# Another opening for a hybrid attention block: x turned by products with a diagonal, and the first key projection by halves of the tokens

## The chip, the cores and the metric

The kernel runs on one core of one Trainium2 chip. The time is device microseconds of one execution, input and output in DRAM; the figure that counts is the median of several runs. One execution of the kernel before was also taken by the hardware profiler, and all rows shown here are of it. The engines are named as in its page: PE (TensorE matmul), PEld (the loading of PE's stationary operand), DVE (VectorE), ACT (ScalarE), POOL (GpSimd) and SP (SyncE, which here only issues DMAs).

## The reference, cut to what matters

The reference is one layer of a block with 512 tokens and 1024 features. The change touches its first steps:

```python
xn = rmsnorm(x, n_mix_pre)           # x * rsqrt(mean(x*x) + eps) per token, times one weight per feature
proj = xn @ w_in                     # 1024 x 14352
qa, ka, va, za, beta_logit, a_dt, qb, kb, vb, gb, gate_a, gate_b = _split_cols(proj, IN_SIZES)
...
qkv = jax.nn.silu(causal_depthwise_conv(jnp.concatenate([qa, ka, va], axis=-1), conv_a))
...
beta = jax.nn.sigmoid(beta_logit)
g = -jnp.exp(a_log) * jax.nn.softplus(a_dt + dt_bias)
```

beta_logit and a_dt are 8 columns each, columns 6144 to 6159 of w_in; the keys ka are columns 1024 to 2047. After these come a gated delta rule over 8 heads, a retention over 4 heads, gates, an output projection and an MLP, all unchanged here.

## The kernel before, in words

Products with weights are made in three parts: each float32 operand is split into a high part of the matmul's own float32r type and a low part that is the rest, and `mm3` (lines 82 to 87) adds high by high, high by low and low by high in PSUM (the lines L84, L85, L86 of the profile). `weights` (L88) issues on SP's queue the load of a block of 512 KB into one of two buffers `raw` (L94), then `split_weights` makes `whi` on ACT (L121) and `wlo` on DVE (L122), each in a ring of three buffers. A block for the keys is 2 groups of 128 features of x by 512 columns, so a block feeds 4 x 2 x 3 = 24 matmuls and four blocks make the first 512 key columns.

The order on each engine is made by a scheduler when the program is built: it follows dependences and priorities, and each engine then runs its own list strictly in that order. The list of SP decides when loads are issued; a load of a block waits until the buffer that it fills has been read.

The opening (L399 to L507) works like this:

- The norm weight of 4 KB goes to one partition (`wrow`, L401), and two float32 matmuls with a row of ones spread it over 128 partitions in two PSUM banks (`wmix`, L406).
- Eight bf16 matmuls on zeros (`warm`, L413) run on PE before data has come.
- SP loads x in four tiles of 128 tokens (L417), then a block of 128 columns from column 6144 for beta and the decay (512 KB, of which 16 columns are used), then the key blocks. ACT's queue loads `cmat` (192 KB: an identity, a triangle and a mask, L419); POOL's queue loads five small tensors (L422 to L427).
- For each pair of tiles ACT squares and sums (L434), and `root` (L375 to L385) makes the norm's factor per token, its square root on ACT at L379, the rest on DVE.
- For each tile DVE makes `xn`, x times factor times weight, in two halves (L444); `rows_to_features` turns it by transposes on PE (L363) four at a time; ACT rounds each four to the high part (L396), DVE makes the low part (L397). The results are the two `actT` tiles, `xs` in the code.
- After each pair the beta/decay matmuls run, 24 of 256 tokens into a PSUM tile of 128 rows (`pba`).
- The chain of beta and decay follows (L463 to L507): a copy on ACT (`baT`, L466), small transposes (L469), exponentials and a logarithm with three table loads on ACT, and tiny DVE steps.
- Then `keys(0, ...)` calls `feature_major` (L287), which runs the four key blocks with 96 matmuls of all 512 tokens. `conv_silu` (L539) takes each of the four results: ACT copies (L544) and scales (L549), DVE makes three taps (L551) and so on. The matmul with `tg` at L575 is the first on PE that does not belong to the first keys or the opening.

`seen` and `passed` (L76) are rows of 48 numbers; each mark is a copy of one number by ACT (L105) and by POOL (L106), after which a DMA that adds in DRAM is issued. From the load numbered 13 on, `weights` also issues DRAM to DRAM copies from a list (`trickle`, L98), one for each load.

Of the kernel before, what the change touches and what calls it, by code (L numbers as in the profile page):

```python
# [10 lines left out]
F32 = mybir.dt.float32  # L11
F32R = mybir.dt.float32r
# [3 lines left out]
ALU = mybir.AluOpType  # L16
# [3 lines left out]
P = 128  # L20
T = 512
D = 1024
# [3 lines left out]
OFF_BA = 6144  # L26
# [34 lines left out]
def hybrid_block_kernel(ctx: ExitStack, tc: tile.TileContext, a: dict, out: bass.AP):  # L61
    nc = tc.nc
# [10 lines left out]
    marks = itertools.count()  # L73
    act = ctx.enter_context(tc.tile_pool(name="act", bufs=2))
    sm = ctx.enter_context(tc.tile_pool(name="sm", bufs=2))
    seen, passed = (sm.tile([1, 48], F32, tag=f"mark{i}", name="mark", bufs=1) for i in range(2))  # L76
    psm = ctx.enter_context(tc.tile_pool(name="psm", bufs=4, space=PSUM))
    psx = ctx.enter_context(tc.tile_pool(name="psx", bufs=4, space=PSUM))
    dr = ctx.enter_context(tc.tile_pool(name="dr", bufs=2, space=DRAM))
# [1 line left out]
    def mm3(ps, lhs, rhs, first, last):  # L81
        lh, ll = lhs
        rh, rl = rhs
        nc.tensor.matmul(ps, lh, rh, start=first, stop=False)  # L84
        nc.tensor.matmul(ps, lh, rl, start=False, stop=False)  # L85
        nc.tensor.matmul(ps, ll, rh, start=False, stop=last)  # L86
# [310 lines left out]
            nc.vector.tensor_tensor(dst[1][:, ks, tt], ps, dst[0][:, ks, tt], ALU.subtract)  # L397

    with tc.tile_pool(name="xp", bufs=2) as xp:  # L399
        wrow = xp.tile([1, D], F32, name="wrow", bufs=1)  # L400
        nc.scalar.dma_start(wrow, a["norm_mix_pre"][0:1, :])  # L401
        one = xp.tile([1, P], F32, name="one", bufs=1)
        nc.vector.memset(one, 1.0)
        wmix = [psm.tile([P, T], F32, tag="mm", name="wmix") for _ in range(2)]
        for half in range(2):
            nc.tensor.matmul(wmix[half], one, wrow[:, half * T : half * T + T], start=True, stop=True)  # L406
        warm = xp.tile([P, T], BF16, name="warm", bufs=1)
        nc.vector.memset(warm, 0.0)
        first = xp.tile([1, 1], F32, name="first", bufs=1)
        nc.scalar.activation(first, one[:, 0:1], AF.Sqrt)  # L410
        pw = psx.tile([P, T], F32, tag="dl", name="dl", bufs=3)
        for _ in range(8):
            nc.tensor.matmul(pw, warm[:, 0:P], warm, start=True, stop=True)  # L413
        xts = []
        for t in range(4):
            xt = xp.tile([P, D], F32, tag="x", name="x", bufs=4)
            nc.sync.dma_start(xt, x_d[t * P : (t + 1) * P, :])  # L417
            xts.append(xt)
        nc.scalar.dma_start(cmat, a["c_mat"])  # L419
# [8 lines left out]
        pba = [psm.tile([P, 256], F32, tag="mm", name="mm") for _ in range(2)]  # L428
        rx = []
        for pair in range(2):  # L430
            v = xp.tile([P, 2], F32, tag="xv", name="xv")
            for i in range(2):
                junk = xp.tile([P, D], BF16, tag="junk", name="junk")
                nc.scalar.activation(junk, xts[2 * pair + i], AF.Square, accum_out=v[:, i : i + 1])  # L434
            nc.vector.tensor_scalar(v, v, 1.0 / D, EPS, ALU.mult, ALU.add)
            y = root(v)
            rx += [y[:, i : i + 1] for i in range(2)]
            if pair == 0:
                wh, wl = weights(w_in, 0, 8, OFF_BA, P)
        for t in range(4):  # L440
            xn = xp.tile([P, D], F32, tag="xn", name="xn")
            for half in range(2):
                hs = slice(half * T, half * T + T)
                nc.vector.scalar_tensor_tensor(xn[:, hs], xts[t][:, hs], rx[t], wmix[half], ALU.mult, ALU.mult)  # L444
            rows_to_features(xn, t, xs)
            if t % 2:
                tt = slice((t - 1) * P, (t + 1) * P)
                for kt in range(8):
                    mm3(
                        pba[t // 2],  # L450
                        (wh[:, kt, :], wl[:, kt, :]),
                        (xs[0][:, kt, tt], xs[1][:, kt, tt]),
                        kt == 0,
                        kt == 7,
                    )
# [4 lines left out]
        nc.vector.tensor_scalar(convw, pv[:, 1, :], 0.5, None, ALU.mult)  # L460
        nc.scalar.copy(later, cmat[:, 2 * P : 3 * P])


        baT = xp.tile([16, T], F32, tag="baT", name="baT")
        for i in range(2):
            nc.scalar.copy(baT[:, i * 256 : i * 256 + 256], pba[i][0:16, :])  # L466
        pb = psx.tile([P, 4, P], F32, tag="tr", name="tr", bufs=1)
        for c in range(4):
            nc.tensor.transpose(pb[:, c, 0:16], baT[:, c * P : (c + 1) * P], ident[0:16, 0:16])  # L469
        ba = xp.tile([P, 4, 16], F32, tag="ba", name="ba")  # L470
        nc.vector.tensor_copy(ba, pb[:, :, 0:16])
        nc.scalar.activation(beta, ba[:, :, 0:8], AF.Exp, scale=-1.0)
# [36 lines left out]
    def gate_rows(pss, o_t, zt):  # L509

# [79 lines left out]
    with tc.tile_pool(name="pa", bufs=1) as pa:  # L590
# [9 lines left out]
        def keys(g4, pool):  # L600
# [700 lines left out]
```

## Time and profile before

| what | value |
|---|---|
| median of 3 runs | 1380.97 us (1379.35, 1380.97, 1384.16) |
| the profiled execution's own time | 1381.27 us |
| its span, first to last instruction | 1379.3 us |
| PE busy | 1357.4 us, 98% of the span |
| DVE, ACT, POOL busy | 953.5, 647.9, 149.0 us |
| DMA | 230.42 MB, mean 167 GB/s |

The profiled execution took 2.0 us more than its span, and lies 0.3 us above the median. In rows of the timeline the first number is the start in us from the span's start, the second the length; what stands in brackets is how long the engine was idle before, and what ended that. Matmuls are pipelined, so the rate of a stream is read from start to start, not from the length of a row. A float32 matmul is recorded twice.

### The profile page before, as it was taken

The page shows a single profiled execution, that of the slowest core. Times are in us where ns is not written, and L with a number is a line of the kernel's source. Part 1 is how long each engine was busy: PE and PEld are TensorE (multiplying, and loading weights), DVE is VectorE, ACT ScalarE, POOL GpSimd, SP SyncE. Part 2 cuts the span into 40 slices and gives each one's busy share as a digit, 9 for nine tenths or more (in the row PEclk, how much of TensorE's full clock was granted, in tenths as well). Part 3 has the DMA queues.
Part 4 walks back from the last instruction along what each step waited for, and adds up shares of the span by engine and source line. Part 5 has one row for each costly group of instructions (what it writes and reads, how often), then busy time and mean ns, then how long its engine had stood idle before and what let it go on. Part 6 is the DMA issues. An engine that isn't in the chain of part 4 may idle for free.

```text
span 1379.3 us, 17789 instructions
## 1 busy us (share of the span) xinstructions
PE 1357.4 (98%) x6574; PEld 1107.1 (80%) x6574; DVE 953.5 (69%) x1631; ACT 647.9 (47%) x1198; POOL 149.0 (11%) x218
## 2 busy tenths in 40 slices
PE   8999999999999999999999999999999999999997
PEld 6888788787887888888888888878878888888885
DVE  5599889963675557567477577575776757395688
ACT  5777564634453323454453343343355544353443
POOL 1112200221012001201001002010001101100000
PEclk9999999999999999999999999999999999999999
DMA  5243625469358447977476477582659847765563
GB/s 161 67 148 108 202 74 170 130 137 237 105 124 173 115 145 201 249 235 193 117 222 158 133 195 147 160 243 77 184 212 293 207 127 223 159 188 162 184 196 123
DMA packets 108281, 230.42 MB, mean 167 GB/s; under 512 B 7616, under 2 KB 21074, under 8 KB 107683
## 3 DMA queue, kind: packets, MB, share of 16 engines
q1 hardware_dynamic: 89424, 177.76, 40.3%
q0 software_dynamic: 18048, 50.29, 19.2%
q10 hardware_dynamic: 722, 1.25, 0.2%
q8 instruction: 51, 0.84, 0.2%
q14 instruction: 36, 0.29, 0.1%
HBM read 221.40 MB, written 74.97 MB: 215 GB/s over the span
## 4 chain that ended last, share of the span: by engine, by line
PE 83%; DVE 8%; DMA 5%; ACT 2%; issue 1%; POOL 1%; SPq 0%; DVEq 0%; ACTq 0%
PE mm L86 17%; PE mm L85 16%; PE mm L84 16%; PE mm L281 13%; PE dl L281 10%; DMA raw<-in_w_in_dram 3%; PE tr L363 2%; DVE wlo L122 1%; ACT whi L121 1%; PE dl L86 1%; PE dl L85 1%; PE dl L84 1%; DVE c_y L551 1%; PE dl L815 1%; DMA raw<-in_w_out_dram 1%
## 5 line engine op out<-in xcount | busy, mean ns | idle before, releaser
L122 DVE TENSOR_TENSOR wlo<-raw,whi 128x1024 fp32r<-128x1024 f32 x262 | 320.0, 1223 | 275.8 <-ACT whi L121 274.1
L121 ACT CAST whi<-raw 128x1024 fp32r<-128x1024 f32 x262 | 275.1, 1051 | 462.5 <-PE mm L85 257.5
L86 PE MATMUL mm<-actT,wlo 128*128 128x512 f32 (+1 forms) x528 | 209.1, 396 | 0.0
L85 PE MATMUL mm<-actT,whi 128*128 128x512 f32 (+1 forms) x528 | 208.0, 394 | 1.0 <-DVE actT L397 1.0
L84 PE MATMUL mm<-actT,whi 128*128 128x512 f32 (+1 forms) x528 | 207.7, 395 | 0.6 <-ACT actT L396 0.6
L84 PEld LDWEIGHTS mm<-actT,whi 128*128 128x128 f32 x528 | 100.5, 191 | 20.5 <-ACT actT L396 1.0
L85 PEld LDWEIGHTS mm<-actT,whi 128*128 128x128 f32 x528 | 100.4, 190 | 20.3 <-DVE actT L397 1.3
L86 PEld LDWEIGHTS mm<-actT,wlo 128*128 128x128 f32 x528 | 100.7, 191 | 18.7
L84 PE MATMUL mm<-hn,whi 128*128 128x512 f32 (+1 forms) x288 | 106.9, 371 | 0.5 <-DVE fr L1200 0.5
L86 PE MATMUL mm<-hn,wlo 128*128 128x512 f32 (+1 forms) x288 | 106.7, 371 | 0.0
L85 PE MATMUL mm<-hn,whi 128*128 128x512 f32 (+1 forms) x288 | 106.6, 370 | 0.0
L84 PE MATMUL mm<-og,whi 128*128 128x512 f32 x256 | 99.8, 390 | 0.3 <-DVE zz L514 0.3
L85 PE MATMUL mm<-og,whi 128*128 128x512 f32 x256 | 99.7, 390 | 0.0
L86 PE MATMUL mm<-og,wlo 128*128 128x512 f32 x256 | 99.7, 390 | 0.0
L281 PE MATMUL mm<-whi,xsum 128*128 128x512 f32 x256 | 82.3, 395 | 0.0
L281 PE MATMUL mm<-whi,fsum 128*128 128x512 f32 x240 | 77.2, 395 | 0.0
L106 POOL COPY mark<-mark 1x1 f32<-1x1 f32 x42 | 33.2, 791 | 395.0 <-ACT mark L105 388.0
L551 DVE SCALAR_TENSOR_TENSOR c_y<-c_raw,convw,c_y 128x512 f32<-128x512 f32 x96 | 70.0, 745 | 3.5 <-ACT c_y L549 2.8
L84 PEld LDWEIGHTS mm<-hn,whi 128*128 128x128 f32 x288 | 54.2, 188 | 10.8 <-issue 0.7
L85 PEld LDWEIGHTS mm<-hn,whi 128*128 128x128 f32 x288 | 54.3, 188 | 10.1
L86 PEld LDWEIGHTS mm<-hn,wlo 128*128 128x128 f32 x288 | 54.2, 188 | 10.0
L84 PE MATMUL mm<-whi,actT 128*128 128x512 f32 x152 | 61.4, 404 | 0.1
(339 smaller groups left out, 2588.0 us busy)
## 6 DMA issues: line engine op xcount, KB each, us to landing
raw<-in_w_in_dram SPq DMA_DIRECT2D x105, 512.0 KB, 3.8
raw<-sums SPq DMA_DIRECT2D x64, 512.0 KB, 4.0
raw<-in_w_up_dram SPq DMA_DIRECT2D x36, 512.0 KB, 6.7
sums<-in_w_in_dram SPq DMA_DIRECT2D x32, 512.0 KB, 5.3
sums<-sums POOLq DMA_DIRECT2D x32, 512.0 KB, 7.7
sums<-in_w_down_dram SPq DMA_DIRECT2D x32, 512.0 KB, 7.1
raw<-in_w_down_dram SPq DMA_DIRECT2D x24, 512.0 KB, 4.5
raw<-in_w_br_a_dram SPq DMA_DIRECT2D x16, 512.0 KB, 4.2
```

What stands on the lines that cost most here:

```text
L84: nc.tensor.matmul(ps, lh, rh, start=first, stop=False)
L85: nc.tensor.matmul(ps, lh, rl, start=False, stop=False)
L86: nc.tensor.matmul(ps, ll, rh, start=False, stop=last)
L106: mark = nc.gpsimd.tensor_copy(passed[:, k : k + 1], seen[:, k : k + 1])
L121: nc.scalar.copy(hi[:, :n], raw[:, :n])
L122: nc.vector.tensor_tensor(lo[:, :n], raw[:, :n], hi[:, :n], ALU.subtract)
L281: m = nc.tensor.matmul(pss[t], lhs[i // 2], rhs[i % 2], start=first and k + i == 0, stop=k + i == 5, skip_group_check=not first,)
L363: nc.tensor.transpose(ps, src, ident)
L551: nc.vector.scalar_tensor_tensor(y, raw[:, j : j + T], tap(j), y, ALU.mult, ALU.add)
L815: nc.tensor.matmul(po[:, hh, :], at[:, 4 * hh + c, :], vn[:, hh, :], start=True, stop=True)
```

## The change

The transposes of the normed x are replaced. The factor of each token is put on the diagonal of a 128 x 128 matrix (`diag`, one DVE operation with the identity), and a float32 matmul with 128 features of x as the stationary operand and that diagonal as the moving one gives the turned and scaled tile. The norm's weight then belongs to the partition: it comes as 8 rows of 128 (`wm_in`), is turned once on PE into a column per group of features (`wcol`), and is applied as a scale when ACT and DVE split the turned tile (`split_from`, 256 tokens at a time, 8 for each pair). `wmix`, `xn` and `rows_to_features` are not used in the opening any more.

The beta/decay weights are loaded as 16 columns (64 KB in pieces of 64 bytes) between the second and the third tile of x; high and low part stand side by side as 32 columns of one stationary operand, so 2 matmuls of 256 tokens take the place of 3, and a DVE addition joins the two halves later. The first keys are made by halves of 256 tokens: three blocks of weights are kept in the ring while the first half runs, the second half follows after the beta/decay matmuls, and the fourth block runs both halves at once. The identity is loaded ahead of the rest of `cmat`, which goes behind x on SP's queue. 16 zero matmuls stand where 8 stood. The rows of marks have 64 numbers. The number of blocks that `weights` counts is one smaller from here on.

```diff
-    seen, passed = (sm.tile([1, 48], F32, tag=f"mark{i}", name="mark", bufs=1) for i in range(2))
+    seen, passed = (sm.tile([1, 64], F32, tag=f"mark{i}", name="mark", bufs=1) for i in range(2))
...
-        wmix = [psm.tile([P, T], F32, tag="mm", name="wmix") for _ in range(2)]
-        for half in range(2):
-            nc.tensor.matmul(wmix[half], one, wrow[:, half * T : half * T + T], start=True, stop=True)
...
+        nc.scalar.dma_start(ident, a["c_mat"][:, 0:P])
...
-        for _ in range(8):
+        for _ in range(16):
             nc.tensor.matmul(pw, warm[:, 0:P], warm, start=True, stop=True)
...
+            nc.sync.dma_start(xts[t], x_d[t * P : (t + 1) * P, :])
+            if t == 1:
+                nc.sync.dma_start(
+                    wba, w_in[:, OFF_BA : OFF_BA + 16].rearrange("(k p) c -> p k c", p=P)
+                )
+        nc.sync.dma_start(cmat[:, P : 3 * P], a["c_mat"][:, P : 3 * P])
...
+                diag = xp.tile([P, P], F32, tag="diag", name="diag", bufs=4)
+                nc.vector.tensor_scalar(diag, ident, y[:, i : i + 1], None, ALU.mult)
...
+                        nc.tensor.matmul(
+                            ps[:, kk, i * P : (i + 1) * P],
+                            xts[2 * pair + i][:, k * P : (k + 1) * P],
+                            diags[i],
...
+                    split_from(ps[:, kk, :], xs[0][:, k, tt], xs[1][:, k, tt], wcol[:, k : k + 1])
...
+        token_features(0)
+        wba2 = xp.tile([P, 8, 32], F32R, name="wba2", bufs=1)
...
+        beta_decay(0)
+        kept = [key_weights(0), key_weights(1)]
+        first_keys(0, kept[0], [0])
+        token_features(1)
...
+        first_keys(1, kept[1], [0])
+        kept.append(key_weights(2))
+        first_keys(2, kept[2], [0])
+        beta_decay(1)
...
+        for k2 in range(3):
+            first_keys(k2, kept[k2], [1])
+        first_keys(3, key_weights(3), [0, 1])
...
-            pss = feature_major(w_in, xs, OFF_KA + g4 * 512, 512, 8)
+            pss = pss or feature_major(w_in, xs, OFF_KA + g4 * 512, 512, 8)
...
-            keys(0, pa2)
+            keys(0, pa2, pk0)
```

ACT's list from the squares of the first two tiles (`junk,xv<-x`) to the last high part of x (`actT`), in the kernel before; `whi` is the rounding of a block of weights:

```order
L434 ACTIVATE junk,xv<-x 128x1024 x2
L461 CAST later<-cmat 128x128
L379 ACTIVATE nr_y<-xv 128x2
L434 ACTIVATE junk,xv<-x 128x1024 x2
L396 CAST actT<-tr 128x4x128
L379 ACTIVATE nr_y<-xv 128x2
L121 CAST whi<-raw 128x1024
L396 CAST actT<-tr 128x4x128 x3
L121 CAST whi<-raw 128x1024 x2
L466 COPY baT<-mm 16x256
L396 CAST actT<-tr 128x4x128 x4
```

The same place in the changed kernel, where the fourth tile's square stands between the first and the second of the first pair's eight splits:

```order
L379 ACTIVATE nr_y<-xv 128x2
L441 ACTIVATE junk,xv<-x 128x1024
L346 ACTIVATE actT<-tr,wcol 128x256
L441 ACTIVATE junk,xv<-x 128x1024
L346 ACTIVATE actT<-tr,wcol 128x256 x3
L121 CAST whi<-raw 128x1024
L346 ACTIVATE actT<-tr,wcol 128x256 x3
L121 CAST whi<-raw 128x1024
L379 ACTIVATE nr_y<-xv 128x2
L502 CAST later<-cmat 128x128
L346 ACTIVATE actT<-tr,wcol 128x256
L121 CAST whi<-raw 128x1024
```

The root of the second pair (the second `nr_y`) has moved behind two roundings of weights and six more splits; the second pair's eight splits follow the third rounding.

PE's list in the kernel before, around the transposes of the second pair's third and fourth tile (`tr<-cmat,xn`); `mm<-actT,whi` of 256 tokens is beta/decay, of 512 tokens the first keys:

```order
L363 MATMUL tr<-cmat,xn 128x128 x12
L469 MATMUL tr<-cmat,baT 128x16 x2
L84 MATMUL mm<-actT,whi 128x256
L84 MATMUL mm<-actT,whi 128x512 x2
L363 MATMUL tr<-cmat,xn 128x128 x4
L84 MATMUL mm<-actT,whi 128x512
L363 MATMUL tr<-cmat,vecs_in 128x128
L85 MATMUL mm<-actT,whi 128x256
```

All but three of the 96 key matmuls of 512 tokens stand behind the last transposes of x.

In the changed kernel `tr<-diag,x` are the products with the diagonal and `mm` of 256 tokens are key matmuls; these rows begin at the last key matmuls ahead of the second pair:

```order
L481 MATMUL mm<-actT,whi 128x256 x2
L481 MATMUL mm<-actT,wlo 128x256
L481 MATMUL mm<-actT,whi 128x256
L455 MATMUL tr<-diag,x 128x128 x12
L481 MATMUL mm<-actT,whi 128x256
L481 MATMUL mm<-actT,wlo 128x256
L481 MATMUL mm<-actT,whi 128x256 x2
L481 MATMUL mm<-actT,wlo 128x256
L481 MATMUL mm<-actT,whi 128x256
L455 MATMUL tr<-diag,x 128x128 x4
```

Ahead of the second pair's products PE now has 31 of the 192 key matmuls of 256 tokens and the first pair's 16 beta/decay matmuls; the other 161 key matmuls stand behind the first twelve products of the second pair.

More of the change, by code (lines that the diff above doesn't have):

```diff
@@ L410, in hybrid_block_kernel @@
         nc.scalar.activation(first, one[:, 0:1], AF.Sqrt)
+        nc.scalar.dma_start(ident, a["c_mat"][:, 0:P])
+        wm_in = xp.tile([8, P], F32, name="wm_in", bufs=1)
+        nc.scalar.dma_start(wm_in, a["norm_mix_pre"][0].rearrange("(k c) -> k c", c=P))
         pw = psx.tile([P, T], F32, tag="dl", name="dl", bufs=3)
-        for _ in range(8):
+        for _ in range(16):
             nc.tensor.matmul(pw, warm[:, 0:P], warm, start=True, stop=True)
-        xts = []
+        xts = [xp.tile([P, D], F32, tag="x", name="x", bufs=4) for _ in range(4)]
+        wba = xp.tile([P, 8, 16], F32, name="wba", bufs=1)
         for t in range(4):
[L416 to L419, printed above, removed]
+            nc.sync.dma_start(xts[t], x_d[t * P : (t + 1) * P, :])
[4 more added lines that the diff above has]
+        nc.sync.dma_start(cmat[:, P : 3 * P], a["c_mat"][:, P : 3 * P])
         vecs_in = xp.tile([P, P], F32, name="vecs_in")
@@ L427, in hybrid_block_kernel, with token_features @@
         nc.gpsimd.dma_start(ab[:, 8:16], a["dt_bias"][0].partition_broadcast(P))
-        pba = [psm.tile([P, 256], F32, tag="mm", name="mm") for _ in range(2)]
-        rx = []
-        for pair in range(2):
+        wcol = xp.tile([P, 8], F32, name="wcol", bufs=1)
+        pv = psx.tile([P, 4, P], F32, tag="dl", name="tr", bufs=3)
+        nc.tensor.transpose(pv[:, 0, 0:8], wm_in, ident[0:8, 0:8])
+        nc.vector.tensor_copy(wcol, pv[:, 0, 0:8])
+        pba = psx.tile([P, 4, P], F32, tag="tr", name="pba", bufs=1).rearrange("p c n -> p (c n)")[0:32, :]
+        pk0 = [psm.tile([P, T], F32, tag="mm", name="mm") for _ in range(4)]
+        def token_features(pair):
             v = xp.tile([P, 2], F32, tag="xv", name="xv")
@@ L436, in hybrid_block_kernel @@
             y = root(v)
[L437 to L454, printed above, removed]
-                    )
+            diags = []
@@ new lines, in token_features @@
+            for i in range(2):
+                diag = xp.tile([P, P], F32, tag="diag", name="diag", bufs=4)
+                nc.vector.tensor_scalar(diag, ident, y[:, i : i + 1], None, ALU.mult)
+                diags.append(diag)
+            tt = slice(2 * pair * P, (2 * pair + 2) * P)
+            for k2 in range(4):
+                ps = psx.tile([P, 2, 256], F32, tag="dl", name="tr", bufs=3)
+                for kk in range(2):
+                    k = 2 * k2 + kk
+                    for i in range(2):
+                        nc.tensor.matmul(
+                            ps[:, kk, i * P : (i + 1) * P],
+                            xts[2 * pair + i][:, k * P : (k + 1) * P],
+                            diags[i],
+                            start=True,
+                            stop=True,
+                        )
+                for kk in range(2):
+                    k = 2 * k2 + kk
+                    split_from(ps[:, kk, :], xs[0][:, k, tt], xs[1][:, k, tt], wcol[:, k : k + 1])
@@ new lines, in beta_decay, with first_keys @@
+        def beta_decay(pair):
+            tt = slice(256 * pair, 256 * pair + 256)
+            for kt in range(8):
+                for i in range(2):
+                    nc.tensor.matmul(
+                        pba[:, tt], wba2[:, kt, :], xs[i][:, kt, tt],
+                        start=pair + kt + i == 0, stop=kt + i == 8, skip_group_check=pair == 1,
+                    )
+        def first_keys(k2, wts, pairs):
+            for f, pair, kk in itertools.product(range(4), pairs, range(2)):
+                tt = slice(256 * pair, 256 * pair + 256)
+                fs = slice(f * P, (f + 1) * P)
+                kt = 2 * k2 + kk
+                for i in range(3):
+                    nc.tensor.matmul(
+                        pk0[f][:, tt], wts[i // 2][:, kk, fs], xs[i % 2][:, kt, tt],
+                        start=pair + kt + i == 0, stop=kt + i == 9, skip_group_check=pair == 1,
+                    )
@@ L456, in hybrid_block_kernel, with key_weights @@
+        def key_weights(k2):
+            return weights(w_in, 2 * k2, 2, OFF_KA, 512)
+        token_features(0)
+        wba2 = xp.tile([P, 8, 32], F32R, name="wba2", bufs=1)
+        nc.scalar.copy(wba2[:, :, 0:16], wba)
+        nc.vector.tensor_tensor(wba2[:, :, 16:32], wba, wba2[:, :, 0:16], ALU.subtract)
+        beta_decay(0)
+        kept = [key_weights(0), key_weights(1)]
+        first_keys(0, kept[0], [0])
+        token_features(1)
         pv = psx.tile([P, 4, P], F32, tag="dl", name="tr", bufs=3)
@@ L461, in hybrid_block_kernel @@
         nc.scalar.copy(later, cmat[:, 2 * P : 3 * P])
[L464 to L467, printed above, removed]
+        first_keys(1, kept[1], [0])
+        kept.append(key_weights(2))
+        first_keys(2, kept[2], [0])
+        beta_decay(1)
+        baT = xp.tile([32, T], F32, tag="baT", name="baT")
+        nc.scalar.copy(baT, pba)
+        pb = psx.tile([P, 4, P], F32, tag="dl", name="tr", bufs=3)
         for c in range(4):
-            nc.tensor.transpose(pb[:, c, 0:16], baT[:, c * P : (c + 1) * P], ident[0:16, 0:16])
+            nc.tensor.transpose(pb[:, c, 0:32], baT[:, c * P : (c + 1) * P], ident[0:32, 0:32])
         ba = xp.tile([P, 4, 16], F32, tag="ba", name="ba")
         nc.vector.tensor_copy(ba, pb[:, :, 0:16])
+        nc.vector.tensor_tensor(ba, ba, pb[:, :, 16:32], ALU.add)
         nc.scalar.activation(beta, ba[:, :, 0:8], AF.Exp, scale=-1.0)
@@ L598, in hybrid_block_kernel, with keys @@
         nc.gpsimd.memset(rt, 0.0)
-        def keys(g4, pool):
+        def keys(g4, pool, pss=None):
             br2 = pool.tile([P, 16], F32, tag="br2", name="br2")
```

2 lines of the change are left out of this document (removed).

## Prediction

> **What bounds the kernel now.** I read the page's first part, the windows, and then the timeline of the first 51 us, engine by engine. First the page and the windows (columns: stretch, length, busy time and count of PE, PEld, DVE, ACT and POOL, granted clock, DMA share, GB/s):
>
> ```profile
> PE 1357.4 (98%) x6574; PEld 1107.1 (80%) x6574; DVE 953.5 (69%) x1631; ACT 647.9 (47%) x1198; POOL 149.0 (11%) x218
> ```
>
> ```profile
> 0.00:25.00 25.00, 20.17 (x73) 13.31 (x74) 13.95 (x31) 13.58 (x24) 4.18 (x13) 1.00 0.59 179
> 25.00:50.00 25.00, 24.96 (x126) 20.70 (x125) 11.85 (x27) 14.78 (x27) 3.53 (x1) 1.00 0.34 99
> 50.00:100.00 50.00, 49.99 (x248) 40.49 (x247) 42.10 (x97) 40.17 (x111) 4.13 (x14) 1.00 0.40 120
> 100.00:150.00 50.00, 47.72 (x239) 39.09 (x237) 48.66 (x129) 36.92 (x108) 10.66 (x11) 1.00 0.47 152
> ```
>
> From 25 us on PE is never idle until the stretch of 100 to 150, where DVE is busy 48.66 of 50. So what the opening can give is how much earlier PE reaches the end of the first keys, as far as DVE comes along. The opening itself, in PE's timeline:
>
> ```profile
> 1.53 2.74 PE L413 MATMUL dl<-warm 128*128 128x512 bf16 x6 [1.53 <-DVE warm L408]
> ...
> 7.91 1.03 PE L413 MATMUL dl<-warm 128*128 128x512 bf16 x2
> 10.44 2.82 PE L363 MATMUL tr<-cmat,xn 128*128 128x128 f32 x12 [1.50 <-DVE xn L444]
> ...
> 16.56 0.42 PE L86 MATMUL mm<-actT,wlo 128*128 128x256 f32 x1
> 16.78 0.42 PE L84 MATMUL mm<-actT,whi 128*128 128x256 f32 x1
> ...
> 24.65 0.60 PE L363 MATMUL tr<-cmat,xn 128*128 128x128 f32 x4
> ...
> 25.56 0.28 PE L86 MATMUL mm<-actT,wlo 128*128 128x256 f32 x1
> 25.68 0.29 PE L84 MATMUL mm<-actT,whi 128*128 128x256 f32 x1
> ...
> 33.08 0.39 PE L85 MATMUL mm<-actT,whi 128*128 128x512 f32 x1
> 33.31 0.39 PE L86 MATMUL mm<-actT,wlo 128*128 128x512 f32 x1
> ...
> 50.61 0.62 PE L575 MATMUL dl<-tg,later 128*128 128x512 f32 x2
> ```
>
> and from the chain of waits (start, length, what), eight records of four float32 matmuls 128 wide:
>
> ```profile
> 54.84 0.89 PE dl L627 x8
> ```
>
> The same matmul of 256 tokens starts every 0.22 us at 16.6 and every 0.12 at 25.6: PE runs at half rate through the first 20 us, though the granted clock in the windows says 1.00 throughout. A key matmul of 512 tokens takes 0.23 (33.08 to 33.31), and the first keys end at 50.6. A float32 matmul 128 wide takes 0.22 at full rate (0.89 over 4), so 0.44 at half rate; a transpose takes half of that (12 in 2.82 at half rate).
>
> **The change part by part.** The second pair's products release most of the key work, so I follow the queue that leads to them, ACT's, then sum what PE still has to do.
>
> ```profile
> 8.55 0.20 ACT L379 ACTIVATE nr_y<-xv 128x2 f32<-128x2 f32 x1
> 9.37 1.06 ACT L434 ACTIVATE junk<-x 128x1024 bf16<-128x1024 f32 x1 [0.62 <-DMA x<-in_x_dram]
> ...
> 10.75 1.06 ACT L434 ACTIVATE junk<-x 128x1024 bf16<-128x1024 f32 x1 [0.23 <-DMA x<-in_x_dram]
> ...
> 12.49 1.04 ACT L121 CAST whi<-raw 128x1024 fp32r<-128x1024 f32 x1
> ...
> 18.38 1.04 ACT L121 CAST whi<-raw 128x1024 fp32r<-128x1024 f32 x1 [2.23 <-DMA raw<-in_w_in_dram]
> 21.50 0.36 ACT L466 COPY baT<-mm 16x256 f32<-16x256 f32 x1 [2.08 <-PE mm L86]
> ...
> 29.23 0.36 ACT L466 COPY baT<-mm 16x256 f32<-16x256 f32 x1
> ...
> 38.22 1.27 ACT L574 ACTIVATE tg<-cmat,glo 128x128 fp32r<-128x128 f32 x4
> ...
> 46.72 0.59 ACT L544 COPY c_raw<-mm 128x512 f32<-128x512 f32 x1 [0.49 <-PE mm L86]
> 47.21 0.69 ACT L549 ACTIVATE c_y<-mm,convw 128x512 f32<-128x512 f32 x1
> ```
>
> ```profile
> 9.64 2.06 DVE L444 SCALAR_TENSOR_TENSOR xn<-x,nr_y,wmix 128x512 f32<-128x512 f32 x3
> ...
> 13.56 1.23 DVE L122 TENSOR_TENSOR wlo<-raw,whi 128x1024 fp32r<-128x1024 f32 x1 [0.16 <-ACT whi L121]
> ...
> 14.78 0.68 DVE L397 TENSOR_TENSOR actT<-tr,actT 128x512 fp32r<-128x512 f32 x1
> ...
> 28.50 0.29 DVE L460 TENSOR_SCALAR convw<-tr 128x128 f32<-128x128 f32 x1 [0.69 <-PE tr L363]
> ```
>
> *x and the small loads.* The 16 columns go ahead of the third tile: 1024 pieces of 64 bytes. No row has this. By bytes it is an eighth of a tile, and the last two tiles came 1.38 apart (9.37 and 10.75): 0.17. By pieces, the old block of 128 columns is 1024 pieces behind the fourth tile on the same queue and was there by 12.49: at most 1.74. I take 1.0 nearer to the pieces, being the same queue and count; both ends stay. The Trainium skill (DMA: Bandwidth & Descriptors, Specifications) says that pieces under 512 bytes run below line rate, which speaks against this edit; by it the upper end would be the one. No run so far shows pieces of 64 bytes on this queue. The rest of `cmat` behind x, the identity ahead of it and the new weight column I cost at nothing: ACT's later work covers them. The root at 8.55 stood behind `later`, which waited for `cmat`; it now stands behind the 16 columns on ACT, so I leave it where it was (a gain or a loss of 1 us, inside the ends above).
>
> *First pair.* With the root at 8.55, DVE's chain to 9.64 and two diagonals at 0.29, products start at about 10.4, where the transposes started. A split of 256 tokens costs ACT between 0.36 (the copy of 256 at 21.50) and 0.69 (the scaled 512 at 47.21); I take 0.44, near the first since half the width decides; DVE 0.40 by the same halving of 0.74 and 0.68. Third square at 9.37 + 1.0 = 10.4, to 11.5 with its readout; one split to 12.0; fourth square (its tile lands 11.75) to 13.2; three splits to 14.5, rounding 1.0 to 15.5; three splits to 16.8, rounding to 17.8; root and `later` 0.5; a split to 18.7. DVE takes the second block's low part (1.23) to 19.1, one split 0.4, four root steps 0.85, a diagonal 0.3: 20.65, and PE starts the second pair at 20.9. The third block cannot hurry it: its buffer is free at 16.8, and a load came 3.6 after that (14.79 to 18.38), so its rounding starts at 20.4, with ACT waiting; the second pair's splits are late by this but PE has keys meanwhile.
>
> *What PE has left at 20.9*, at full rate: 16 products at 0.22 = 3.6; 161 key matmuls of 256 at 0.119 = 19.2 (two of 256 cost 0.01 more than one of 512, some 1 us in all); 16 beta/decay matmuls = 1.9, where before 24 stood; small transposes and the two 32-wide products 1.2. Sum 25.9, end 46.8 against 50.6: 3.8 earlier. The fourth block's low part is due at 41.2 and ready by 37.5, so the kept ring costs nothing; without that slack its 2.2 us would show.
>
> *What comes along.* The chain of beta and decay starts when the second pair's beta/decay matmuls end: 20.9 + 3.6 + 41 keys (4.9) + 0.3 + 1.9 = 31.6. From its copy at 29.23 to the end of `tg` at 39.49 it took 10.26 before. Now two roundings more wait in the midst of it for kept buffers (2.0) and one stands behind it: ACT takes the first key result at 44.6, not at 43 when PE has it; before, 46.72. So DVE's work on the keys starts 2.1 earlier, PE's list 3.8. Later DVE binds:
>
> ```profile
> 127.40 0.63 PE L363 MATMUL tr<-cmat,kf 128*128 128x128 f32 x4 [0.83 <-DVE kf L555]
> ...
> 149.95 0.33 PE L363 MATMUL tr<-cmat,c_y 128*128 128x128 f32 x1 [1.45 <-DVE c_y L555]
> ```
>
> At these two waits PE's lead over DVE is given back, so the gain lies between 2.1 and 3.8; I take 3.0.
>
> *No effect:* the marks,
>
> ```profile
> L106 POOL COPY mark<-mark 1x1 f32<-1x1 f32 x42 | 33.2, 791 | 395.0 <-ACT mark L105 388.0
> ```
>
> are 42 single numbers as before; longer rows move later tiles by 128 bytes, which no row prices, and POOL idles anyway. That the load count is one lower moves each DRAM copy one block later; with DMA at 0.34 to 0.47 in these stretches I put this at 0, plus or minus 1.
>
> The sum against the profiled execution: 1381.27 - 3.0 = 1378.3; it lies 0.3 above the median, so the median goes to 1378.0.
>
> **The rivals.** *PE stays at half rate (slower).* Before, PE reached full rate only after unbroken matmuls from 16.2 to past 21; the eight zero matmuls did not do it. Now 16 of them fill 1.53 to 8.4 (0.43 each), then PE idles to 10.4 and has short gaps to 16. If the rate is still half when the second pair starts, keys and beta/decay ahead of it take 0.21 each, the products come 2 to 4 us late, and each us at half rate after that costs about 0.45. Half rate until 16: end of keys at 49.2, gain 1.4. Until 22: 51.3, loss 0.7. Until 25: 52.6, loss 2.0, time 1383.0. It decides against the change from about 21. (Until 16, each of the first four groups of products takes 1.75 for 0.89, and the second pair starts at 23.2; until 22, the 47 matmuls ahead of it cost 4.4 more, and it starts at 25.3; 25.9 follow.) For it: the row at 16.6. Against: 6.9 us without a gap, and float32 products where transposes stood. The Trainium skill (TensorE: Matmul & The Clock Gate, Part 1) says about 3.4 us of sustained activity bring the full clock and an idle window of that length takes it away; by that rule the 16 suffice and the gap of 2 us does not undo them. The trace agrees in part: 6.9 us of matmuls and one-row products (1.53 to 8.9) did not bring it.
>
> *DVE follows and the small load is free (faster).* With the 16 columns at 0.17 and splits at 0.36 (15 of them ahead, 1.2 us), the second pair starts at 18.9 and both ends move by 2 more: 5 earlier, 1376.0. For it: ACT bounds this stretch, not PE.
>
> *The time saved is lost again.* From 50 on ACT and DVE have the same work in another order; if they hold their dates, PE stands 3 us longer at the two waits above: 1381. Against: their dates hang on the first key result.
>
> **How the numbers follow.** The forecast gets 0.52, half rate 0.17, the faster case 0.24, the absorbed one 0.07. 0.3%, 4.1 us, is about what a measurement of this kernel tells from no change: under 1376.8 counts as faster, over 1385.1 as slower. Faster: the whole faster case and 0.10 of the forecast's own spread, 0.34. Slower: half rate past 27 or together with a late x, 0.07. Same: 0.59. The range takes in the faster case with 2 us for the unpriced order and copies, and half rate to 25: 1374.0 to 1383.0.
>
> **What would show it.** Right: the `tg` product (first foreign matmul) near 46.8; the second pair's products at 20.9; key matmuls of 256 tokens every 0.12 from 16 on; the first `c_raw` copy near 44.6; the wait that is 1.45 now, grown. Wrong: 0.21 from start to start past 20, a third tile after 11.2, or a later end of DVE's stretch though the keys end sooner.

## The result, and the profile after

The changed kernel takes 1369.69 us (median of 4 runs), the kernel before 1382.57 us beside it (4 runs): a ratio of 0.9907, with a 95% interval of 0.988 to 0.9934. That is 12.9 us, where 3.0 were forecast; the time lies 4.3 us below the range. The 12.9 is probably on the high side: two near twins of the changed kernel among the experiments (8 zero matmuls, blocks counted from 1) gained 10.5 and 9.9 us beside their own runs of the kernel before. The profiled execution took 1371.24 us, its span 1369.1 against 1379.3.

PE's line of the page, and three of the windows shown before:

```profile
PE 1346.4 (98%) x6691; PEld 1111.3 (81%) x6691; DVE 952.5 (70%) x1637; ACT 650.0 (47%) x1205; POOL 150.7 (11%) x218
...
0.00:25.00 25.00, 21.03 (x132) 16.69 (x132) 12.46 (x36) 15.21 (x31) 4.18 (x13) 0.93 0.63 194
25.00:50.00 25.00, 24.19 (x195) 23.38 (x194) 15.78 (x33) 15.35 (x30) 3.52 (x1) 1.00 0.24 74
...
100.00:150.00 50.00, 48.95 (x247) 40.11 (x246) 49.27 (x139) 39.75 (x118) 14.75 (x16) 1.00 0.50 155
```

PE has 11.0 us less busy time in a span that is 10.2 shorter: the time went out of PE's work, not out of its waits. The opening in the timelines of PE and ACT:

```profile
1.53 5.78 PE L411 MATMUL dl<-warm 128*128 128x512 bf16 x16 [1.53 <-DVE warm L403]
9.89 4.29 PE L455 MATMUL tr<-diag,x 128*128 128x128 f32 x24 [2.43 <-DVE diag L447]
20.85 2.84 PE L455 MATMUL tr<-diag,x 128*128 128x128 f32 x24
48.02 0.62 PE L623 MATMUL dl<-tg,later 128*128 128x512 f32 x2
```

```profile
9.96 1.06 ACT L441 ACTIVATE junk<-x 128x1024 bf16<-128x1024 f32 x1 [1.33 <-DMA x<-in_x_dram]
...
43.90 0.59 ACT L592 COPY c_raw<-mm 128x512 f32<-128x512 f32 x1
```

The second pair's products start at 20.85, the first `tg` product at 48.02 (before 50.61) and ACT takes the first key result at 43.90 (before 46.72). This is much like the opening that was forecast. Where the rest comes from shows when the start of the same matmul is read in both traces all along (before, after, difference in us):

```
62.34    59.61   -2.73   product on kf (the 16th record)
309.31   306.38  -2.93
422.74   420.62  -2.12
439.23   440.75  +1.52   recurrence, product with vn and kd
585.85   587.44  +1.59
1032.39  1029.16 -3.24   first matmuls on hn
1186.46  1180.39 -6.07
1364.75  1354.92 -9.83
```

The lead of the opening is lost at one place near 430, and then PE gains 11.35 us to the end. Most of it comes bit by bit. The one step is near 1001, where two short waits of the kernel before (0.30 at 1001.35 and 0.76 at 1002.61, some 1.6 us with the slower start after them) are missing in the changed one. In PE's groups of the kernel before they are the idle time in the last column:

```profile
L84 PE MATMUL mm<-keep,actT 128*128 128x512 f32 x40 | 16.0, 400 | 0.3 <-ACT keep L121 0.3
L85 PE MATMUL mm<-keep,actT 128*128 128x512 f32 x40 | 15.9, 397 | 0.8 <-DVE keep L122 0.8
```

Such a wait stands at this place in some profiles of either opening (0.64 us with the longer rows alone, 0.76 with the blocks counted from 1), so it is not put down to the change. The groups of PE's instructions, shapes kept apart, show what is faster (count, busy time, mean ns of one, idle time before); the kernel before, then the changed one:

```profile
L84 PE MATMUL mm<-og,whi 128*128 128x512 f32 x256 | 99.8, 390 | 0.3 <-DVE zz L514 0.3
L84 PE MATMUL mm<-hn,whi 128*128 128x512 f32 x224 | 88.5, 395 | 0.0
L281 PE MATMUL mm<-whi,xsum 128*128 128x512 f32 x256 | 82.3, 395 | 0.0
```

```profile
L84 PE MATMUL mm<-og,whi 128*128 128x512 f32 x256 | 99.8, 390 | 0.5 <-DVE zz L562 0.5
L84 PE MATMUL mm<-hn,whi 128*128 128x512 f32 x224 | 87.1, 389 | 0.0
L281 PE MATMUL mm<-whi,xsum 128*128 128x512 f32 x256 | 80.8, 389 | 0.0
```

The same 128 x 128 x 512 matmul took 390 ns on `og` and 395 on `hn` or `xsum` before; after, these groups all take 389 to 390. From start to start the difference is as large, 5.5 ns. The timeline of the kernel before has 18 matmuls in 4.18 us, 0.2322 each, and that of the changed kernel 24 in 5.44, 0.2267 each:

```profile
1058.89 0.39 PE L86 MATMUL mm<-hn,wlo 128*128 128x512 f32 x1
...
1063.07 0.40 PE L86 MATMUL mm<-hn,wlo 128*128 128x512 f32 x1
```

```profile
1058.22 0.39 PE L85 MATMUL mm<-hn,whi 128*128 128x512 f32 x1
...
1063.66 0.39 PE L85 MATMUL mm<-hn,whi 128*128 128x512 f32 x1
```

Summed from start to start over the whole trace, matmuls on `hn` take 4.1 us less, those on `xsum` and `fsum` 2.3 each, those on the kept weights (`keep`) 2.1: 10.8 of the 11.35 us. Of the 2.1, some 1.6 are the two waits above; so what the rate alone gives is near 9.2. Nothing in the opening touches these tiles. They belong to pools that are placed after `sm`, and `sm` holds the two rows of marks: 64 numbers instead of 48, two rows, move every later tile by 128 bytes in each partition. In the built programs the weights `whi` and `wlo` and the tiles `actT`, `og` and `q` begin at 32 modulo 256 bytes in both kernels; `hn`, `xsum` and `fsum` begin at 160 before and at 32 after, and so do five of the seven `keep` tiles.

The loss near 430 (PE's and ACT's timelines, then the window of 430 to 435; before, then after):

```profile
430.34 1.05 ACT L121 CAST whi<-raw 128x1024 fp32r<-128x1024 f32 x1 [3.82 <-DMA raw<-in_w_in_dram]
...
432.39 1.13 PE L795 MATMUL dl<-vn,kd 128*128 128x256 f32 x4 [0.69 <-ACT vn L790]
...
430.00:435.00 5.00, 4.31 (x23) 3.29 (x22) 3.23 (x5) 3.05 (x5) 0.00 (x0) 1.00 0.93 245
```

```profile
430.34 1.04 ACT L121 CAST whi<-raw 128x1024 fp32r<-128x1024 f32 x1 [7.33 <-DMA raw<-in_w_in_dram]
...
432.39 1.92 PE L843 MATMUL dl<-vn,kd 128*128 128x256 f32 x4 [2.80 <-ACT vn L838]
...
430.00:435.00 5.00, 2.61 (x9) 2.13 (x10) 2.54 (x3) 2.36 (x4) 0.00 (x0) 0.76 0.90 221
```

The block of weights lands at the same date in both, so a lead of 2.1 us becomes a wait (2.80 against 0.69): ACT's list has the rounding of that block ahead of `vn`. After the longer idle time the granted clock is 0.50 from 432.6 to 436.0 (0.76 over the window shown), and the difference moves from 0 at 432.39 to +1.52 at 439.23. Not every execution loses so much here: in three other profiles of the new opening (rows of 48, 8 zeros, blocks counted from 1) the wait for `vn` is 0.98 to 1.07 us, its product starts at 429.86, 430.68 and 430.77, and the clock stays at 1.00.

### The profile page after: what moved, and what is told of

It is laid out like the page before. It is cut to its first block, busy times and chain, and to the rows that moved or that the text cites. A ratio compares the mean times of both kernels' runs of the same rounds, so it can differ in the third digit from the quotient of the medians.

```text
span 1369.1 us, 18032 instructions
## 1 busy us (share of the span) xinstructions
PE 1346.4 (98%) x6691; PEld 1111.3 (81%) x6691; DVE 952.5 (70%) x1637; ACT 650.0 (47%) x1205; POOL 150.7 (11%) x218
## 4 chain that ended last, share of the span: by engine, by line
PE 86%; DVE 6%; DMA 3%; ACT 3%; issue 1%; POOL 1%; SPq 0%; DVEq 0%; ACTq 0%
PE mm L84 16%; PE mm L86 16%; PE mm L85 16%; PE mm L281 12%; PE dl L281 10%; PE tr L363 2%; DMA raw<-in_w_in_dram 2%; PE mm L481 2%; DVE wlo L122 1%; PE dl L86 1%; PE dl L863 1%; PE dl L85 1%; PE dl L84 1%; PE dl L843 1%; PE dl L835 1%
## 5 line engine op out<-in xcount | busy, mean ns | idle before, releaser
L85 PE MATMUL mm<-actT,whi 128*128 128x512 f32 x480 | 190.5, 397 | 0.0
L86 PE MATMUL mm<-actT,wlo 128*128 128x512 f32 x480 | 189.9, 397 | 0.0
L84 PE MATMUL mm<-actT,whi 128*128 128x512 f32 x480 | 189.8, 396 | 0.0
L84 PEld LDWEIGHTS mm<-actT,whi 128*128 128x128 f32 x480 | 90.3, 188 | 18.6 <-ACT c_y L597 0.8
L86 PEld LDWEIGHTS mm<-actT,wlo 128*128 128x128 f32 x480 | 90.5, 189 | 17.7
L85 PEld LDWEIGHTS mm<-actT,whi 128*128 128x128 f32 x480 | 90.2, 188 | 17.6
L281 PE MATMUL dl<-whi,actT 128*128 128x512 f32 x192 | 61.1, 389 | 0.0
```

What stands on the lines that cost most here:

```text
L281: m = nc.tensor.matmul(pss[t], lhs[i // 2], rhs[i % 2], start=first and k + i == 0, stop=k + i == 5, skip_group_check=not first,)
```

## The experiments

Ratios are against the kernel before, run beside each.

### What places do

Two kernels divide the change: the old kernel with the new rows, as here, and the new kernel with the old rows, the reverse.

```diff
-    seen, passed = (sm.tile([1, 48], ...
+    seen, passed = (sm.tile([1, 64], ...
```

> The kernel before with rows of marks of 64 numbers and nothing else. Theory P (place in memory): all tiles of the later stages move by 128 bytes, and the 512-column matmuls on hn, xsum and fsum go from 0.232 to 0.227 us from start to start; some 1440 of them and the output projection make 8 to 11.5 us, so 1369.5 to 1374. Rival O (the opening and what follows from it did it, the marks do nothing): no change, within 1 us of the kernel before.

> The changed kernel with rows of marks of 48 numbers again, all else as changed. Theory P: matmuls on hn, xsum and fsum go back to 0.232 us; the opening's 2.3 us are all that is left, and the wait near 430 us eats them: 0 to 3 us under the kernel before, 1379 to 1383. Rival O: all of the gain stays, 1368 to 1372.

Measured: 1370.17 us, ratio 0.9933 (0.9915 to 0.9951), for the longer rows alone; 1378.09 us, 0.9984 (0.9974 to 0.9994), for all the rest. So the longer rows are worth 9.2 us (6.8 to 11.7), which is what the rates gave, and the opening 2.2 (0.8 to 3.6); together 11.4, inside the interval of the change. The second time lies 0.9 below theory P's 1379, but inside its 0 to 3 us under the kernel before. Rival O is gone.

Whether one address or the distance of two counts: 128 bytes ahead of all tiles, without and with the longer rows.

```diff
     cp = ctx.enter_context(tc.tile_pool(name="cp", bufs=1))
+    nc.gpsimd.memset(cp.tile([P, 32], F32, name="pad"), 0.0)
```

> The kernel before with 128 bytes ahead of all tiles (and one memset on POOL for them): every tile moves by 128 bytes, and the distance between any two stays. Theory P1 (what counts is the distance between the two operands of a matmul, modulo 256 bytes): hn, xsum, fsum stay at 0.232 us, actT and q at 0.227, time within 1.5 us of the kernel before. Rival P2 (what counts is the address of one operand by itself): hn, xsum, fsum go to 0.227 us and gain 8 to 11.5 us, while the matmuls on actT go to 0.232 and lose up to 8 in the first 450 us.

> The kernel before with 128 bytes ahead of all tiles and rows of marks of 64 numbers as well: all operands stand at the place modulo 256 that was the slow one for hn before. Theory P1 (distance of the operands): all 512-column matmuls at 0.227 us, 8 to 11.5 us faster than the kernel before, as with the longer rows alone. Rival P2 (address by itself): all at 0.232 us, hn and actT alike, 0 to 8 us slower than the kernel before.

Measured: 1381.02 us, 1.001 (0.9997 to 1.0022), and 1370.64 us, 0.9931 (0.9914 to 0.9948). PE's groups in the two:

```profile
L84 PE MATMUL mm<-og,whi 128*128 128x512 f32 x256 | 99.7, 390 | 0.4 <-DVE zz L514 0.4
L84 PE MATMUL mm<-hn,whi 128*128 128x512 f32 x224 | 88.5, 395 | 0.0
```

```profile
L84 PE MATMUL mm<-og,whi 128*128 128x512 f32 x256 | 99.8, 390 | 0.5 <-DVE zz L514 0.5
L84 PE MATMUL mm<-hn,whi 128*128 128x512 f32 x224 | 87.2, 389 | 0.0
```

In the first, `hn` stands at 32, the place where it is fast in the changed kernel, and is slow; in the second all operands stand at 160, where `hn` was slow, and all are fast. The address of one operand by itself decides nothing. The kernel before already held a case of it: `vr` and `s` both stand at 160, like the slow `hn`, and their matmul takes the short time.

```profile
L84 PE MATMUL dl<-vr,s 128*128 128x512 f32 x40 | 15.6, 390 | 0.0
```

To show that the partner is the weights, their ring alone was moved:

```diff
     ring = ctx.enter_context(tc.tile_pool(name="ring", bufs=3))
+    nc.gpsimd.memset(ring.tile([P, 32], F32, tag="pad", name="pad", bufs=1), 0.0)
     act = ctx.enter_context(tc.tile_pool(name="act", bufs=2))
+    nc.gpsimd.memset(act.tile([P, 32], F32, tag="pad", name="pad", bufs=1), 0.0)
```

> The kernel before, in which only the rings of weights (raw, whi, wlo) move by 128 bytes against everything else modulo 256 (two memsets on POOL more). Theory P1 (distance of the two operands): whi and wlo now stand apart from actT, og and q and in step with hn, xsum and fsum: the former go from 0.227 to 0.232 us (some 3000 matmuls, 15 us lost), the latter from 0.232 to 0.227 (8 us gained); 1385 to 1392, slower than the kernel before. Rival P3 (hn, xsum and fsum are slow for where they stand against something else than the weights): no change, 1378 to 1382.

Measured: 1383.55 us, 1.0023 (1.0011 to 1.0034), and the groups have changed places:

```profile
L84 PE MATMUL mm<-og,whi 128*128 128x512 f32 x256 | 101.1, 395 | 0.1
L84 PE MATMUL mm<-hn,whi 128*128 128x512 f32 x224 | 87.1, 389 | 0.0
L281 PE MATMUL mm<-whi,xsum 128*128 128x512 f32 x256 | 80.9, 389 | 0.0
```

`og`, `actT` and `q` are now the slow ones and lose 12.7 us from start to start (4.2, 7.0, 1.5), `hn`, `xsum` and `fsum` gain 8.3. The sign and the rate are as forecast (from start to start, the medians of the three slow groups go from 227 to 232 ns). The time is not: it lies below the 1385 to 1392 of theory P1 and above the 1378 to 1382 of rival P3. On `actT` the 512-column intervals under 300 ns grow by 11.4 us, but the longer ones, which hold PE's waits, shrink by 4.1. Then other distances:

```diff
+e6: sm.tile([1, 80], ...   e7: sm.tile([1, 56], ...   e16: sm.tile([1, 72], ...   e15: rows of 56 and 64
```

> The kernel before with rows of marks of 80 numbers: the later tiles move by 256 bytes instead of 128. If only the distance modulo 256 counts, hn, xsum and fsum stay at 0.232 us and the time stays, 1378 to 1382. If the longer row itself, or room ahead of the later tiles, were the cause, it would gain 8 to 11 us as rows of 64 did.

> The kernel before with rows of marks of 56 numbers: the later tiles move by 64 bytes, and the operands on hn, xsum and fsum stand 192 bytes apart modulo 256. If any distance other than 0 costs, 0.232 us and no change (1378 to 1382); if only a distance of 128 does, 0.227 and 8 to 11 us faster; in between if it goes by the distance.

> The kernel before with rows of marks of 56 and of 64 numbers: the later tiles move by 96 bytes, and hn, xsum and fsum stand 32 bytes from being in step with the weights (distance 224 modulo 256). If the cost goes by the distance, a small one as here costs little, 0.227 to 0.229 us; if it is all or nothing, 0.232.

> The kernel before with rows of marks of 72 numbers: the later tiles move by 192 bytes, and hn, xsum and fsum stand 96 bytes from the weights modulo 256. If the cost goes by the distance, near the 0.232 us of 128; if only multiples of 128 count or the sign does, something else, as with the 192 of rows of 56, where part of the matmuls stood at 0.229 and part at 0.232.

The last text miscounts: a move of 192 bytes makes the distance 64 modulo 256, not 96. Measured: rows of 80 (distance 128 again) 1379.75 us, 1.0002 (0.999 to 1.0014); rows of 56 (distance 192) 1376.21, 0.9971 (0.9958 to 0.9983); one run each at distance 224 (1382.06) and 64 (1379.91). The groups of the last three, in the order 192, 224, 64:

```profile
L84 PE MATMUL mm<-hn,whi 128*128 128x512 f32 x224 | 88.5, 395 | 0.0
L281 PE MATMUL mm<-whi,xsum 128*128 128x512 f32 x256 | 81.0, 390 | 0.0
```

```profile
L84 PE MATMUL mm<-hn,whi 128*128 128x512 f32 x224 | 88.6, 396 | 0.0
L281 PE MATMUL mm<-whi,xsum 128*128 128x512 f32 x256 | 82.3, 395 | 0.0
```

```profile
L84 PE MATMUL mm<-hn,whi 128*128 128x512 f32 x224 | 87.9, 393 | 0.0
L86 PE MATMUL mm<-hn,wlo 128*128 128x512 f32 x224 | 87.1, 389 | 0.0
L281 PE MATMUL mm<-whi,xsum 128*128 128x512 f32 x256 | 82.5, 396 | 0.0
```

A move of 256 changes nothing, so neither the longer row nor the room counts, only the distance modulo 256. Distance 0 is the only one of five at which every group is fast; 32 bytes off (224) costs as much per matmul as 128, and at 64 to either side only some pairs are slow. It does not go by the size of the distance.

### What becomes of the opening's lead

The adding DMAs in DRAM fill the stretch in which the lead was lost; three of them follow each other on POOL's queue at 415.31 (the changed kernel, POOL's timeline):

```profile
415.31 3.80 POOL L112 DMA_DIRECT2D sums<-in_w_in_dram  x3
```

First, another order:

```diff
-((2, 0), (1, 0), (3, 0), (2, 2), (1, 2), (3, 2), (0, 0), (0, 2))
+((2, 0), (1, 0), (0, 0), (3, 0), (2, 2), (1, 2), (0, 2), (3, 2))
```

> The changed kernel with the adding DMAs of each block of sums in another order, so that those that read weights no longer run three in a row on POOL's queue. Theory Q (in the changed kernel the block of weights that lands at 430.3 us is late because three such adds are issued from 415.3 to 419.1 and fill the DMA engines): that block lands 1 to 3 us earlier, PE waits under 1.5 us for vn instead of 2.80, the granted clock stays at 1.00 there; 1 to 3 us faster than the changed kernel, 1366 to 1369. Rival (the engines are full there by the bytes alone, whatever the order): the same wait, 1368.5 to 1371.

Measured: 1378.24 us, 0.998 (0.9967 to 0.9993), by the ratios some 10 us slower than the changed kernel and 7 to 8 slower than its two near twins; neither expectation had that. Two windows, and PE's longest wait of the whole:

```profile
320.00:340.00 20.00, 15.21 (x67) 12.44 (x67) 6.63 (x9) 7.92 (x15) 2.05 (x2) 0.91 1.02 209
430.00:435.00 5.00, 5.00 (x27) 4.21 (x25) 3.66 (x5) 1.52 (x2) 0.39 (x1) 1.00 0.92 213
...
PE dl L843 <- ACT vn L838: 5.4, 2, 4.8
```

Near 430 no wait is left (PE busy 5.00 of 5.00, clock 1.00), as theory Q had it. But this does not show that the order did it, since PE comes there 6.4 us later: the product on `og` that starts at 420.62 in the changed kernel starts at 427.03. The order holds for both bursts, and in the earlier one the same kind of wait, now 4.8 us, ends at 333.16, where the changed kernel has 1.20; the granted clock falls to 0.91 over these 20 us. With another order the wait stands at the earlier burst, and theory Q stays untested. So the bursts were spread:

```diff
-                    add_blocks(pool_marks[-1], 8 + 2 * g2)
+                    now = list(itertools.islice(adds, 8 + 2 * g2))
+                    if g2 == 1:
+                        for k in range(1, 14, 2):
+                            trickle[k][1].append(now.pop(0))
+                    trickle.extend(([], [p]) for p in now)
```

> The changed kernel in which the 22 adding DMAs between 286 and 458 us are no longer issued in two bursts behind a mark on POOL, but one with each block of weights (a mark by ACT and POOL ahead of each, as in the later stages). Theory Q2 (the adds cost PE time only where several run at once and hold up a block of weights, near 326 and near 430 us): no wait of PE over 1 us between 300 and 450, granted clock 1.00 there; 2 to 4 us faster than the changed kernel, 1366 to 1368. Rival (the extra marks stand on ACT ahead of its work and the adds only meet other blocks): within 1 us of the changed kernel or slower, 1369 to 1373.

Measured: 1364.73 us, 0.9889 (0.9876 to 0.9902), the fastest of all. Two windows of the changed kernel, then of this one:

```profile
320.00:340.00 20.00, 18.80 (x91) 15.07 (x90) 9.72 (x15) 11.07 (x24) 4.36 (x4) 1.00 1.02 226
...
420.00:430.00 10.00, 9.59 (x45) 7.66 (x43) 3.88 (x5) 1.05 (x1) 0.00 (x0) 1.00 1.06 188
```

```profile
320.00:340.00 20.00, 20.00 (x98) 16.14 (x96) 9.75 (x15) 11.69 (x26) 1.52 (x2) 1.00 0.63 182
420.00:430.00 10.00, 10.00 (x49) 8.14 (x48) 6.47 (x8) 4.34 (x8) 4.71 (x7) 1.00 0.83 161
```

This is below the 1366 to 1368 of theory Q2, whose signs all stand: PE waits nowhere for more than 1 us between 300 and 450, at a clock of 1.00. PE is never idle in these two windows, and the share of the DMA engines is 0.63 and 0.83 instead of 1.02 and 1.06. The traces of the two differ by 6.2 us, all of it gained between 320 and 440. Part of that is the long wait of this one profile of the changed kernel; beside the two near twins, run on the same chip, the gain is 4.8 and 5.4 us by the ratios.

Does the old opening then cost what the new one gains? The kernel before with rows of 64 and the same paced adds; and once more with the blocks counted from -1, so that adds stand with the same blocks:

```diff
-    loads = itertools.count()
+    loads = itertools.count(-1)
```

> The kernel before, with its own opening, but with rows of marks of 64 numbers and the adding DMAs paced one by one as in the run before. It differs from that run (1364.73) by the opening and what belongs to it alone. Theory A (the opening's lead is no longer lost near 330 and 430 us when no block is late there): 2 to 4 us slower than the changed kernel with paced adds, 1366.5 to 1368.5. Rival (the lead is lost at other waits on DVE in any case): within 1 us of it, 1364 to 1366.

> As the run before it, with the old opening, rows of 64 and paced adds, but the blocks counted from -1, so that copies and adds stand with the same blocks as in the changed kernel with paced adds (1364.73). Theory A (no wait near 290, and the opening's lead reaches the end): 1366.5 to 1368.5, with no wait of PE over 1 us between 280 and 450. Rival B (the opening's lead is lost elsewhere): 1364 to 1366. Rival C (the loss near 290 has nothing to do with the place of the adds): 1371 to 1374 again.

Measured: 1372.92 us, 0.9943 (0.9928 to 0.9958), and 1373.29 us, 0.9958 (0.9944 to 0.9972): no faster than the rows of 64 alone (0.9933), so with the old opening the pacing gains nothing. Both expectations of the first missed; by its number the second is rival C. But its trace has the same wait as the first, which had 2.23 us there (POOL's rows of the second, then PE's):

```profile
282.90 0.58 POOL L112 DMA_DIRECT2D sums<-sums  x1
287.25 1.76 POOL L682 DMA_DIRECT2D rn<-scr  x3 [0.29 <-POOL rn L678]
...
292.48 0.66 PE L697 MATMUL dl<-rn,acc 32*32 32x32 f32 x16 [2.08 <-DMA rn<-scr]
```

Here the add and the loads of `rn` are 4.4 us apart, and PE waits 2.08 us for `rn`. With the new opening and the paced adds (1364.73 us) they are 8 us apart, and PE has no such wait; POOL's rows there:

```profile
277.19 0.59 POOL L112 DMA_DIRECT2D sums<-sums  x1
285.14 1.76 POOL L730 DMA_DIRECT2D rn<-scr  x3 [0.29 <-POOL rn L726]
```

In the first run's profile (1377.39 us, the slowest of its six executions) the granted clock was 0.50 from 292 to 305 behind this wait, in the second's (1369.80, the fastest of its six) 1.00. So the pacing brings a wait of its own with the old opening; that the nearness of the add causes it is read from the rows and was not tested. This pair of runs doesn't measure the opening. The figure for it stays the 2.2 us of the kernel with rows of 48.

### Zero matmuls and the count

```diff
-        for _ in range(16):
+        for _ in range(8):
```

> The changed kernel with 8 zero matmuls at the beginning instead of 16. Theory C (16 of them bring PE to full rate before the first products; 8 do not, as in the kernel before): the first pair's products take 0.22 each instead of 0.11 and key matmuls of 256 tokens 0.21 to 0.22 until unbroken work has run for some us; the first keys end 1 to 2.5 us later, and the time is 0.5 to 2.5 us longer than the changed kernel's, 1370 to 1372. Rival (the products alone bring the rate, the zeros do nothing): products at 0.11 within 1 us of their start, no change.

Measured: 1369.78 us, 0.9924 (0.9912 to 0.9936). In PE's timeline:

```profile
1.53 3.59 PE L411 MATMUL dl<-warm 128*128 128x512 bf16 x8 [1.53 <-DVE warm L403]
9.37 4.59 PE L455 MATMUL tr<-diag,x 128*128 128x128 f32 x24 [3.71 <-DVE diag L447]
14.15 1.05 PE L455 MATMUL tr<-diag,x 128*128 128x128 f32 x8
```

The first 24 records of the products take 4.59 us with 8 zeros and 4.29 with 16 (2.84 at full rate), and both are at full rate from 14 on. The time is within 0.4 us of the 1370.11 of its twin with 16 zeros (the next run below). Theory C falls; the zeros are not what makes the opening faster. In two other profiles with 16 zeros (rows of 48, shown here, and the other order of the adds) the products ran at full rate at once; whether the zeros did that was not tested.

```profile
9.42 2.94 PE L455 MATMUL tr<-diag,x 128*128 128x128 f32 x24 [2.05 <-DVE diag L447]
```

Then the count of the blocks:

```diff
-    loads = itertools.count()
+    loads = itertools.count(1)
```

> The changed kernel with the blocks of weights counted from 1, so that each copy in DRAM is issued with the same block as in the kernel before. If the copies' place matters for the wait near 430 us or elsewhere: 1 to 3 us to either side of the changed kernel. If not, as the prediction had it (0 plus or minus 1): 1368.5 to 1371.

Measured: 1370.11 us, 0.9928 (0.9908 to 0.9948): the count does nothing that can be measured. The wait near 430 is 1.03 us in its profile instead of 2.80, but it is 1.07 with 8 zeros and the old count too, so this is not put down to the count.

## Why the prediction was wrong

The step that failed is "No effect: the marks". It said that the longer rows move later tiles by 128 bytes, "which no row prices", and put nothing. Rows of the trace of before had a price for the same matmul with its operands in other places, and the prediction does not use them: the groups by shape give 390 ns on `og` and 395 on `hn`, `xsum` and `fsum`. That place was the reason could not be read from them; the runs showed it. 1440 such matmuls at 5.5 ns are 7.9 us; summed from start to start they gain 8.7, and the run of the rows alone gained 9.2. The range should have held a gain of this size: a move of one operand of 1440 matmuls that no row prices is a term without bounds, not a term of nothing.

The other steps, which the kernel with rows of 48 measured alone (forecast 3.0, measured 2.2 with an interval of 0.8 to 3.6, so the opening was forecast within the noise):

- *Second pair at 20.9*: 20.85. *Small load 1.0 us*: the third square came 0.6 later than before (9.37 to 9.96). *First key result at 44.6*: 43.90. All within 0.7. That the pair starts within 0.05 of its date is partly luck: in the six profiles of the new opening it starts between 19.78 and 21.73, and the third square between 9.96 and 10.52.
- *Keys end at 46.8*: the first `tg` product stands at 48.02, so 2.6 of the 3.8 us; PE was idle for 0.8 of the stretch from 25 to 50 (24.19 of 25.00), where the sum had it busy throughout. One pair of profiles is a rough measure here: `tg` starts at 47.10 to 49.12 in the six profiles of the new opening and at 48.25 to 50.61 in the eleven of the old, and the means, 48.0 and 49.9, are 1.9 apart.
- *The two DVE waits take part of the lead back*: they didn't. The wait of 1.45 that was to grow is gone (PE busy 48.95 of 50 from 100 to 150, before 47.72), and the lead was 2.9 at 309.
- *Lost again*: the rival had the right kind and the wrong place. What holds its date is not DVE but a block of weights behind full DMA engines near 430 (DMA share 1.06 from 420 to 430). This profiled execution lost 3.6 there, more than the three others named above. That the trace gains 10.2 and the medians 12.9 fits: it is the slowest of its four executions, and the profiled one of the kernel before (1381.27) lies 1.3 below its median.
- *Each DRAM copy one block later, 0 plus or minus 1*: with the blocks counted from 1 the time was 1370.11, so nothing that can be measured.
- *Half rate*: it came, but ended early. The 16 zeros took 5.78 us and not 6.9; after the idle time of 2.43 us behind them, which was not to undo them, the granted clock was 0.50 from 10 to 12 and 1.00 again from 13. The first 24 records of the products took 4.29 where 2.84 is the full rate; that is 1.5 us at a place where ACT is the limit, the second pair started on its date all the same, and 8 zeros or 16 made no difference. Key matmuls of 256 tokens start every 0.12 us from 16 on, as the signs had it.

## What to carry to other kernels

When a change moves tiles in memory, look for the same instruction with two durations in the groups by shape: a difference of 1.4% over 1400 matmuls was worth four times the edit that the change was about. Keep the two operands of a 512-column float32r matmul in step, that is at the same offset modulo 256 bytes; other types were not run. And follow a lead gained early to the next place where the DMA engines are full: here a block of weights set the date. Spreading the traffic was worth 5 us more with the new opening and nothing with the old, so such a step has to be measured with the kernel that it is meant for.

## What the runs showed of the hardware

- The rate of a 128 x 128 x 512 float32r matmul depends on the distance of its two operands in the partition: 0.227 us at distance 0 modulo 256, 0.232 to 0.233 at 128 and 224, mixed at 64 and 192. 256-column matmuls on `hn` lost nothing: medians of 0.119 to 0.120 at 0 and 128, 0.113 to 0.118 at the other three. The Trainium skill (TensorE: Matmul & The Clock Gate, Part 2, the step by step) says that streaming and loading of weights have read ports of their own, so that the load of the next weights takes nothing from the running matmul. The runs show that something in this pair does interfere; that it is the load of the next weights against the stream was only supposed and not tested, and the measurement decides for the size.
- How long an idle time has to be for the granted clock to fall does not come out as one number. After 2.80 us near 430 it was 0.50 for 3.4 us, after 1.82 at the same place (rows of 72) 0.53 from 434 to 437, after 2.23 near 292 (the first run with the old opening and paced adds) 0.50 from 292 to 305. Idle times of 0.69 to 1.67 near 430 in eleven other profiles, and of 2.08 near 292 in the second such run, left it at 1.00.
- Rows of 56 gained 4.0 us by the ratio (2.3 to 5.8); the groups on `xsum` and `fsum` explain 2.8 from start to start, the rest stays open. How the distance acts stays open too.
